# Sums of squares by row on ScalarE, and key stores on ScalarE's queue, in the first stage of a hybrid attention kernel

## The chip, the cores and the metric

One core of a Trainium2 chip runs the whole layer as one program. The metric is device time in microseconds, the median of several executions; a lower time is better. The engines are TensorE (PE, with its weight loads PEld), VectorE (DVE), ScalarE (ACT), GpSimd (POOL) and SyncE (SP, which here only issues DMAs). Each engine works through its own list in program order and stands still when the next instruction has to wait.

## The reference

The layer takes 2048 latent tokens `x` and 256 context tokens `ctx`, each of width 1024. What matters here is its first part:

```python
def _rmsnorm(x, g):
    xf = x.astype(jnp.float32)
    xf = xf * lax.rsqrt(jnp.mean(xf * xf, axis=-1, keepdims=True) + EPS)
    return (xf * g.astype(jnp.float32)).astype(x.dtype)
...
        h_lat = _rmsnorm(x, norm_g[i]) * (1.0 + scale) + shift
        h_ctx = _rmsnorm(ctx, norm_g[i]) * (1.0 + scale_c) + shift_c
```

`shift` and `scale` come from a product of SiLU(c) with `w_ada`. The normalised and modulated tokens `h` are multiplied by the input projection `w_in` (queries, keys, values and gates of two groups of heads), then come neighbourhood attention, retention, the output projection, a residual and a last RMSNorm.

## The kernel before, in words

Tokens are held transposed: width on the partitions, tokens along the free dimension. They come in nine groups of 256 (0 to 7 are latent, 8 is the context), and two groups make a block of 512 (`blk[0]` to `blk[3]`; `blk[4]` is the context alone, 256 wide). A float32 value is carried as a high part (rounded by ScalarE to `fp32r`) and a low part (the difference, by VectorE or POOL), and each product is three matmuls: high by high, high by low, low by high.

The first stage, some 170 us, does two things at once. PE runs five windows (`window(b)`, L491), one for each block, in which it computes the keys of neighbourhood attention: four key units (`u_k`, L380) of 128 output columns, each with eight k-steps of three matmuls (`tform`, L357; the matmul is L363). A window so has 32 steps, and step n of window b has the number 32b + n. In the first window the four units are interleaved as `STEPS` says; in the others they come one after another. When a unit ends, ScalarE rounds its result into a tile `o` (L383), VectorE forms the low part (L384), and both are stored to DRAM in `kS` (L385). The pool `op` has two buffers for `o`. `store` (L149) defers the DMA by one `tick`, and the window calls `tick` right behind the unit's end, in the same step.

Between the steps stands the preparation of later blocks. `PLAN` (L39) lists it by hand, with the step after which each action is emitted, in the order of the list. For a group i, the actions are: `x`, load the transposed tokens (`load_x`, L182); `sq`, squares on ScalarE (L198), folded from eight k-tiles to one by adds on POOL and VectorE (L200, L201, L203); `cs`, the sum over the partitions by matmuls with a column of ones (L209); `rs`, r = (mean + eps)^-0.5, a scale on VectorE (L214) and a power on POOL (L215), and its copy to 128 columns on VectorE (L220); `sp`, the spread of r over the partitions by matmuls with the identity (L227); `mu`, the tokens times r, on VectorE in halves of four k-tiles (L241); `ab`, times scale plus shift, two k-tiles on VectorE (L272) and two on ScalarE (L274) for most groups; `hl`, the high part on ScalarE (L279) and the low part on VectorE or POOL as `LOV` says (L283). For groups 0 and 1, `p` does the last two by k-tile (`prep_first`, L255: L262 on ScalarE, L263 and L265). `s`, `m`, `ar` and `af` make the four quarters of `scale` and `shift` (L298, L311, L319, L324 to L332). Prepared tokens are also spilled to DRAM in `hS` for later stages (L253, on SP's queue, eight steps behind `hl`), and from there they come back at L516.

The pool `st` has four buffers of 128x1024 float32. They hold the raw weights of `ws` (`st_halves`, L172), the squares of groups 2 to 8 and the raw tokens of group 8, in turn. SP's queue carries all loads, the spills and, up to the last window, the key stores; in window 4 the queue for the stores becomes ScalarE's (L495).

Of the kernel before, what the change touches and what calls it, by code (L numbers as in the profile page):

```python
# [9 lines left out]
F32 = mybir.dt.float32  # L10
BF16 = mybir.dt.bfloat16
F32R = mybir.dt.float32r
AF = mybir.ActivationFunctionType
# [69 lines left out]
def hybrid_kernel(ctx: ExitStack, tc: tile.TileContext, a: dict, out: bass.AP):  # L83
# [47 lines left out]
    env = dict(pp=pool(psx, "pp", 6, space=PSUM), st=pool(sx, "st", 4, side="right"), queue=nc.sync)  # L131
# [61 lines left out]

    def squares(i):
        sqs[i] = []
        for u in range(2):
            sq = xsq[i][u] if i < 2 else env["st"].tile([P, KH, 256], F32, name="st")
# [7 lines left out]
    def colsum(*ii):  # L205
        pm = ptile(None if ii[0] < 4 else psm)
        for j, i in enumerate(ii):
            for t in range(2):
                nc.tensor.matmul(pm[:, 2 * j + t:2 * j + t + 1], sqs[i][0][:, 0, t * P:(t + 1) * P], one, start=True, stop=True)  # L209
            rms[i] = pm[:, 2 * j:2 * j + 2]  # L210

    def rstd(i):
        r = env["st"].tile([P, 2], F32, name="rs", bufs=4)
        nc.vector.tensor_scalar(r, rms[i], 1.0 / D, EPS, ALU.mult, ALU.add)  # L214
# [3 lines left out]
    def spread_copy(i):  # L218
        rbs[i, 1] = env["st"].tile([P, 2, P], F32, name="t0", bufs=2)
        nc.vector.tensor_copy(rbs[i, 1], rbs[i].unsqueeze(2).to_broadcast([P, 2, P]))  # L220
# [95 lines left out]
    def ada_row(u):  # L316
        rows[u] = op.tile([P, 2, 512], F32, name="o")[:, 0, :]
        n = 4 if SPL[u] else 2
        (nc.scalar.copy, nc.vector.tensor_copy)[u % 2](rows[u][0:n, :], aps[u][0:n, :])  # L319
# [1313 lines left out]
```

## Time and profile before

| what | us |
|---|---|
| median of 3 runs (1350.23 to 1353.26) | 1350.68 |
| the profiled execution | 1347.8 |
| its span | 1345.9 |
| PE busy | 1304.7 |
| PEld busy | 1145.7 |
| DVE busy | 834.6 |
| ACT busy | 606.3 |
| POOL busy | 578.9 |

The profile is of one execution. A row of a timeline gives the start, the length, the engine, the line, the operation and its tiles, and in brackets how long the engine had stood before it and what ended that. A row of the groups gives the count, the busy time and the mean in ns, and behind the second bar the idle time ahead of the group by what ended it. A row of the waits gives who waited for whom: us in total, times, longest.

### The profile page before, as it was taken

What the parts mean: (1) busy time and instruction counts of PE and PEld (TensorE: products, weight loads), DVE (VectorE), ACT (ScalarE), POOL (GpSimd) and SP (SyncE); (2) the same over time, 40 slices, a digit from 0 to 9 for tenths busy, and PEclk for the clock granted to TensorE, in tenths of its full rate; (3) what the DMA queues carried; (4) which work ended last, traced back from release to release, by engine and by line L of the source; (5) the groups of instructions that cost most, each with busy time, mean ns of one, the idle gap of its engine ahead of it and who ended that gap; (6) DMA issues with size and microseconds to landing.
All of it is one profiled execution on the core that took longest, in us unless ns stands there. A gap on an engine that the chain in (4) does not pass through costs nothing.

```text
span 1345.9 us, 23104 instructions
## 1 busy us (share of the span) xinstructions
PE 1304.7 (97%) x8236; PEld 1145.7 (85%) x8236; DVE 834.6 (62%) x1444; ACT 606.3 (45%) x1259; POOL 578.9 (43%) x569
## 2 busy tenths in 40 slices
PE   6989999999999999999999999999999999999997
PEld 2477899878898888998999889889999788888886
DVE  5786356776676754477767777776654734444445
ACT  5454333243533343555655465556642244333432
POOL 5452102555104664354535465655533154544442
PEclk9999999999999999999999999999999999999999
DMA  9386788565867657967587876766547888445533
GB/s 363 139 281 235 266 301 219 185 223 184 315 184 230 213 177 239 265 199 198 146 227 210 225 225 205 192 183 192 167 149 250 277 297 275 158 157 172 165 127 125
DMA packets 172086, 287.26 MB, mean 213 GB/s; under 512 B 17345, under 2 KB 92225, under 8 KB 170690
## 3 DMA queue, kind: packets, MB, share of 16 engines
q1 hardware_dynamic: 139554, 228.35, 56.2%
q10 hardware_dynamic: 32416, 57.42, 11.9%
q8 instruction: 66, 1.08, 0.3%
q14 instruction: 50, 0.41, 0.1%
HBM read 194.48 MB, written 91.23 MB: 212 GB/s over the span
## 4 chain that ended last, share of the span: by engine, by line
PE 79%; DVE 6%; DMA 5%; ACT 3%; POOL 3%; issue 2%; SPq 0%; ACTq 0%; POOLq 0%; DVEq 0%
PE mm L374 21%; PE mm L671 17%; PE mm L1474 11%; PE mm L363 7%; PE sS L1034 5%; PE tr L1061 3%; PE po L1082 3%; PE mm L1196 2%; PE tr L1063 2%; PE po L1084 2%; PE mm L311 2%; PE mm L1386 1%; PE mm L1385 1%; PE mm L1384 1%; DMA v<-rvS 1%
## 5 line engine op out<-in xcount | busy, mean ns | idle before, releaser
L374 PE MATMUL mm<-whi,hlo 128*128 128x256 f32 x832 | 228.5, 282 | 1.0 <-DMA hlo<-cS 1.0
L374 PE MATMUL mm<-whi,hhi 128*128 128x256 f32 x768 | 224.2, 292 | 0.0
L374 PE MATMUL mm<-wlo,hhi 128*128 128x256 f32 x768 | 216.8, 282 | 0.0
L1065 ACT CAST pt<-tr 128x640 fp32r<-128x640 f32 (+1 forms) x128 | 95.7, 747 | 160.0 <-PE tr L1063 157.4
L1071 DVE TENSOR_TENSOR pt<-tr,pt 128x640 fp32r<-128x640 f32 (+1 forms) x128 | 113.9, 890 | 78.7 <-ACT pt L1065 77.5
L374 PEld LDWEIGHTS mm<-whi,hlo 128*128 128x128 f32 x832 | 156.5, 191 | 1.4 <-DMA hlo<-cS 1.3
L1054 POOL TENSOR_SCALAR sp<-sp,stt 128x640 f32<-128x640 f32 (+2 forms) x128 | 103.7, 812 | 106.3 <-DVE stt L1053 77.3
L374 PEld LDWEIGHTS mm<-whi,hhi 128*128 128x128 f32 x768 | 146.3, 190 | 0.1
L374 PEld LDWEIGHTS mm<-wlo,hhi 128*128 128x128 f32 x768 | 146.1, 190 | 0.0
L625 POOL TENSOR_TENSOR whi<-st,whi 128x512 fp32r<-128x512 f32 x48 | 64.6, 1367 | 160.2 <-ACT whi L624 159.3
L1043 DVE CUSTOM_DVE_ANT_0 sp<-sS,nb 128x640 f32<-128x640 f32 (+2 forms) x128 | 105.6, 825 | 34.1 <-PE sS L1034 27.7
L1048 ACT ACTIVATE sp<-sp,stt 128x640 f32<-128x640 f32 (+2 forms) x128 | 107.4, 839 | 20.0 <-DVE stt L1043 18.8
L363 PE MATMUL mm<-hhi,whi 128*128 128x512 f32 x256 | 107.4, 419 | 0.0
L363 PE MATMUL mm<-hlo,whi 128*128 128x512 f32 x256 | 101.1, 395 | 6.4 <-DVE hlo L283 2.3
L1034 PE MATMUL sS<-k,q 128*128 128x256 f32 (+3 forms) x512 | 99.1, 315 | 5.3 <-DVE stt L1043 5.1
L363 PE MATMUL mm<-hhi,wlo 128*128 128x512 f32 x256 | 101.2, 395 | 0.3 <-DVE wlo L347 0.3
L671 PE MATMUL mm<-hhi,whi 128*128 128x512 f32 x336 | 97.4, 394 | 0.0
L1474 PE MATMUL mm<-wor,y 128*128 128x512 f32 x384 | 95.6, 398 | 1.3 <-DVE xt L1483 1.2
L1483 DVE TENSOR_TENSOR xt<-mm,xt 128x512 f32<-128x512 f32 x64 | 43.8, 686 | 82.7 <-PE mm L1474 82.7
L1034 PEld LDWEIGHTS sS<-k,q 128*128 128x128 f32 x512 | 82.7, 188 | 12.3 <-DVE stt L1043 8.6
L1474 PE MATMUL mm<-won,y 128*128 128x512 f32 x336 | 89.9, 406 | 0.0
L1474 PEld LDWEIGHTS mm<-wor,y 128*128 128x128 f32 x384 | 69.9, 188 | 17.4 <-issue 3.4
(258 smaller groups left out, 3034.8 us busy)
## 6 DMA issues: line engine op xcount, KB each, us to landing
st<-in_w_in_dram SPq DMA_DIRECT2D x64, 512.0 KB
q<-qS SPq DMA_DIRECT2D x64, 256.0 KB
hlo<-hS SPq DMA_DIRECT2D x20, 512.0 KB
k<-kS SPq DMA_DIRECT2D x16, 576.0 KB
kS<-o SPq DMA_DIRECT2D x16, 512.0 KB
vB<-o SPq DMA_DIRECT2D x64, 128.0 KB
qS<-o ACTq DMA_DIRECT2D x16, 512.0 KB
woS<-g ACTq DMA_DIRECT2D x32, 256.0 KB
```

What stands on the lines that cost most here:

```text
L363: nc.tensor.matmul(pm[:, :n], ww[:, k, cs], h[:, k, :], start=(k == 0 and i == 0), stop=(k == KC - 1 and i == 2))
L374: nc.tensor.matmul(pm[:, t * WG:(t + 1) * WG], h[:, k, o:o + P], ww[:, k, :], start=(k == 0 and i == 0), stop=(k == KC - 1 and i == 2))
L625: nc.gpsimd.tensor_tensor(t[:, 1], r, f(t)[:, 0], ALU.subtract)
L671: nc.tensor.matmul(pm, ww[:, k, :], hh[:, k, :], start=(k == 0 and i == 0), stop=(k == KH - 1 and i == 2))
L1034: nc.tensor.matmul(o, hd["q"][i][:, hl, j * P:(j + 1) * P], k, start=(hl == 0), stop=(hl == 1))
L1043: nc.vector.tensor_tensor_reduce(T["sp"][:, :n], T["s"], nbz[big][:, o:o + n], -1.0, 3e38, ALU.add, ALU.min, T["st"][:, 0:1])
L1048: nc.scalar.activation(sp[:, :n], sp[:, :n], AF.Exp, bias=st[:, 0:1], scale=-1.0, accum_out=st[:, 1:2])
L1054: nc.gpsimd.tensor_scalar(sp[:, :n], sp[:, :n], st[:, 2:3], 0.0, ALU.mult, ALU.add)
L1065: nc.scalar.copy(pt[:, :ng_ + 2, 0, :], tr[:, :ng_ + 2, :])
L1071: nc.vector.tensor_tensor(pt[:, :n, 1, :], tr[:, :n, :], f(pt)[:, :n, 0, :], ALU.subtract)
L1474: nc.tensor.matmul(pm, yy[:, k, :], ww[:, k, sl], start=(k == 0 and i == 0), stop=(k == 3 and i == 2))
L1483: nc.vector.tensor_tensor(xts[t][:, sl], pm, xts[t][:, sl], ALU.add)
```

## The change

Its own summary reads: "Row-wise sums of squares on ScalarE for groups two to eight, with five and six in ScalarE's gap, r on POOL, and key stores on ScalarE's queue one unit later."

For groups two to eight the sum of squares is taken by rows. A new action `xt` loads the group's tokens a second time, untransposed, as two tiles of 128 tokens by 1024, into the buffers of `st`; `squares` is then one ScalarE instruction for each tile, which squares in place and accumulates along the row into a column of `rms`. The folding adds and the column sums of these groups are gone. The scale of `rstd` and the copy of `spread_copy` go from VectorE to POOL for these groups. The rows `ar` of quarters two and three are copied by VectorE (quarter two was ScalarE's). Key stores go on ScalarE's queue in all windows. `PLAN` is written anew: groups two and three load and are squared a few steps from where they were, groups four to eight are squared earlier (five and six at step 18, between the two halves of groups two and three), and the preparation of groups two and three moves from steps 16 to 29 to steps 14 to 22.

```diff
-    (12, 'p', 5), (12, 'm', 3, 1), (12, 'p', 4), (13, 'sq', 4), (13, 'cs', 2, 3), (13, 'm', 3, 2), (14, 'm', 3, 3),
-    (15, 'rs', 2), (15, 'ar', 3), (16, 'rs', 3), (16, 'af', 3), (16, 'sp', 2, 3), (17, 'mu', 3, 0), (18, 'p', 7),
...
+    (-1, 'p', 1), (-1, 'm', 1, 3), (-1, 'ws', 1), (0, 'ar', 1), (3, 'af', 1), (4, 'xt', 2), (4, 'xt', 3), (4, 'mu', 1, 1),
+    (4, 's', 2, 0), (4, 'x', 4), (4, 'p', 2), (7, 'm', 2, 0), (8, 'm', 2, 1), (9, 'p', 3), (9, 'sq', 2), (9, 'sq', 3),
+    (9, 'm', 2, 2), (9, 'm', 2, 3), (9, 'ar', 2), (10, 'xt', 4), (10, 'x', 5), (11, 'xt', 5), (12, 'mu', 0, 1),
+    (12, 'af', 2), (12, 'm', 3, 0), (12, 'p', 5), (12, 'm', 3, 1), (12, 'p', 4), (12, 'rs', 2), (12, 'rs', 3),
+    (13, 'm', 3, 2), (13, 'm', 3, 3), (13, 'ar', 3), (14, 'sp', 2, 3), (14, 'mu', 2, 0), (14, 'mu', 3, 0), (14, 'sq', 4),
+    (14, 'blk', 1), (15, 'xt', 6), (16, 'af', 3), (17, 'rs', 4), (17, 'p', 7), (18, 'p', 6), (18, 'x', 6),
+    (18, 'ab', 2, 0), (18, 'ab', 3, 0), (18, 'hl', 2, 0), (18, 'hl', 3, 0), (18, 'sq', 5), (18, 'sq', 6),
+    (18, 'mu', 2, 1), (18, 'mu', 3, 1), (19, 'ab', 2, 1), (20, 'ab', 3, 1), (21, 'hl', 2, 1), (22, 'hl', 3, 1),
+    (26, 'sp', 4), (28, 'mu', 4, 0), (30, 'mu', 4, 1), (30, 'rs', 5), (30, 'rs', 6), (30, 'xt', 7), (36, 'ab', 4, 0),
+    (38, 'x', 7), (41, 'sq', 7), (42, 'ab', 4, 1), (44, 'rs', 7), (45, 'blk', 2), (46, 'hl', 4, 1), (46, 'hl', 4, 0),
+    (46, 'xt', 8), (50, 'sp', 5), (50, 'x', 8), (51, 'mu', 5, 0), (52, 'mu', 5, 1), (53, 'ab', 5, 0), (54, 'ab', 5, 1),
+    (55, 'hl', 5, 0), (55, 'blk', 3), (58, 'hl', 5, 1), (61, 'sq', 8), (68, 'sp', 6), (70, 'rs', 8), (73, 'mu', 6, 1),
...
-    env = dict(pp=pool(psx, "pp", 6, space=PSUM), st=pool(sx, "st", 4, side="right"), queue=nc.sync)
+    env = dict(pp=pool(psx, "pp", 6, space=PSUM), st=pool(sx, "st", 4, side="right"), queue=nc.scalar)
...
+    def load_xt_(i):
+        sqs[i] = []
+        src = a["ctx"] if i == 8 else a["x"][i * 256:(i + 1) * 256, :]
+        for t in range(2):
+            xt = env["st"].tile([P, KH, 256], F32, name="st").rearrange("p k t -> p (k t)")
+            nc.sync.dma_start(xt, src[t * P:(t + 1) * P, :])
+            sqs[i].append(xt)
+
     def squares(i):
+        if i >= 2:
+            rms[i] = env["st"].tile([P, 2], F32, name="rs", bufs=4)
+            for t, xt in enumerate(sqs[i]):
+                nc.scalar.activation(xt, xt, AF.Square, accum_out=rms[i][:, t:t + 1])
+            return
...
-        nc.vector.tensor_scalar(r, rms[i], 1.0 / D, EPS, ALU.mult, ALU.add)
+        r = rms[i] if i >= 2 else env["st"].tile([P, 2], F32, name="rs", bufs=4)
+        (nc.gpsimd if i >= 2 else nc.vector).tensor_scalar(r, rms[i], 1.0 / D, EPS, ALU.mult, ALU.add)
...
-        nc.vector.tensor_copy(rbs[i, 1], rbs[i].unsqueeze(2).to_broadcast([P, 2, P]))
+        (nc.gpsimd if i >= 2 else nc.vector).tensor_copy(rbs[i, 1], rbs[i].unsqueeze(2).to_broadcast([P, 2, P]))
...
-        (nc.scalar.copy, nc.vector.tensor_copy)[u % 2](rows[u][0:n, :], aps[u][0:n, :])
+        (nc.scalar.copy, nc.vector.tensor_copy)[u > 0](rows[u][0:n, :], aps[u][0:n, :])
...
-            if b == 4 and n == 0:
-                env["queue"] = nc.scalar
```

More of the change, by code (lines that the diff above doesn't have):

```diff
@@ L192, in hybrid_kernel @@
     sqs, rms, rbs, prs = {}, {}, {}, {}
-    def squares(i):
+    def load_xt_(i):
[5 more added lines that the diff above has]
+            sqs[i].append(xt)
+    def squares(i):
+        if i >= 2:
[3 more added lines that the diff above has]
+            return
         sqs[i] = []
         for u in range(2):
-            sq = xsq[i][u] if i < 2 else env["st"].tile([P, KH, 256], F32, name="st")
+            sq = xsq[i][u]
             nc.scalar.activation(sq, raw[i][u], AF.Square)
@@ L205, in colsum @@
     def colsum(*ii):
-        pm = ptile(None if ii[0] < 4 else psm)
+        pm = ptile()
         for j, i in enumerate(ii):
@@ L212, in rstd @@
     def rstd(i):
-        r = env["st"].tile([P, 2], F32, name="rs", bufs=4)
-        nc.vector.tensor_scalar(r, rms[i], 1.0 / D, EPS, ALU.mult, ALU.add)
+        r = rms[i] if i >= 2 else env["st"].tile([P, 2], F32, name="rs", bufs=4)
+        (nc.gpsimd if i >= 2 else nc.vector).tensor_scalar(r, rms[i], 1.0 / D, EPS, ALU.mult, ALU.add)
         nc.gpsimd.tensor_tensor(r, r, mhalf[:, 0:2], ALU.pow)
@@ L466, in hybrid_kernel @@
         lds[name](*args)
-    acts = dict(sq=squares, cs=lambda *i: colsum(*i), rs=lambda i: (rstd(i), spread_copy(i)), sp=lambda *i: spread(*i),
+    acts = dict(sq=squares, xt=load_xt_, cs=lambda *i: colsum(*i), rs=lambda i: (rstd(i), spread_copy(i)), sp=lambda *i: spread(*i),
                 mu=lambda i, u: spread_mul(i, (u,)), ab=prep_ab, hl=prep_hl, blk=alloc_blk, x=load_x, w=lambda: wr.append(w_raw(2560)),
```

20 rows, old and new, of the table PLAN are left out of this document.

## The prediction

> **What bounds the kernel now.** I read the page's busy shares first, then the windows of the first 170 us (the only stretch that the diff touches), then who TensorE (PE) waited for in that stretch, and last the timelines of the engines around each of those waits.
>
> ```profile
> span 1345.9 us, 23104 instructions
> PE 1304.7 (97%) x8236; PEld 1145.7 (85%) x8236; DVE 834.6 (62%) x1444; ACT 606.3 (45%) x1259; POOL 578.9 (43%) x569
> ```
> PE is busy 97% of the span, so only what shortens PE's own list or its few holes can help. The holes lie early:
> ```profile
> 27.00:72.00 45.00, 42.19 (x166) 23.51 (x165) 34.32 (x61) 22.66 (x36) 22.41 (x20) 1.00 0.43 171
> 72.00:100.00 28.00, 24.20 (x111) 19.55 (x111) 24.71 (x33) 14.64 (x20) 14.63 (x8) 1.00 0.98 328
> ```
> The columns are PE, PEld, DVE, ACT, POOL, clock, DMA share, GB/s. From 72 to 100 us VectorE is busy 24.7 of 28 and the DMA engines 98%; ScalarE (ACT) has about half its time free. PE's waits from 27 to 170 us:
> ```profile
> PE mm L363 <- DVE hlo L283: 2.3, 2, 2.0
> ...
> PE mm L227 <- DVE t L220: 1.5, 1, 1.5
> PE mm L363 <- POOL hlo L283: 1.5, 1, 1.5
> PE mm L374 <- DVE wlo L347: 0.8, 1, 0.8
> PE mm L374 <- ACT whi L345: 0.6, 1, 0.6
> ```
> These rows hold 6.7 us. A block of 512 tokens cannot start before its low parts (L283) are written, so preparation sets these stretches, one "gate" at the second half of block 1 and one at the start of block 2:
> ```profile
> 77.43 0.47 PE L363 MATMUL mm<-hlo,whi 128*128 128x512 f32 x1 [0.39 <-DVE hlo L283]
> ...
> 99.62 0.50 PE L363 MATMUL mm<-hlo,whi 128*128 128x512 f32 x1 [1.46 <-POOL hlo L283]
> ...
> 105.06 0.71 PE L227 MATMUL mm<-ident,t 128*128 128x128 f32 x4 [1.50 <-DVE t L220]
> 105.52 0.48 PE L363 MATMUL mm<-hhi,whi 128*128 128x512 f32 x1
> ```
> The question is when these gates open in the changed kernel.
>
> **Part 1: the column sums go from PE.** L209 over groups two to eight:
> ```profile
> L209 PE MATMUL mm<-one,st 128*128 128x1 f32 x28 | 3.6, 237 | 0.4 <-DVE st L203 0.4
> ```
> At most 4.0 us. But five of the seven groups' sums (two to six) lie ahead of the 99.62 gate; if that gate opens when preparation is done, they are absorbed. Only seven and eight, behind it, are sure: 8 of 28 matmuls (about 1.0) with the 0.4 of waiting and some 0.2 of restart, **-1.6 us**.
>
> **Part 2: VectorE and POOL are relieved.**
> ```profile
> L200 DVE TENSOR_TENSOR st<-st 128x512 f32<-128x512 f32 x7 | 5.7, 819 | 0.9 <-ACT st L198 0.9
> L241 DVE TENSOR_TENSOR hlo<-hlo,mm 128x1024 f32<-128x1024 f32 x4 | 4.8, 1213 | 0.5 <-PE mm L227 0.5
> ...
> L201 DVE TENSOR_TENSOR st<-st 128x256 f32<-128x256 f32 x7 | 3.8, 547 | 0.2
> L220 DVE COPY t<-rs 128x256 f32<-128x256 f32 x7 | 3.1, 445 | 5.7 <-POOL rs L215 5.7
> ```
> ```profile
> L201 POOL TENSOR_TENSOR st<-st 128x256 f32<-128x256 f32 x7 | 5.8, 830 | 0.5
> ```
> VectorE loses L200, L201 and L220: 12.6 us of work and 6.8 of waiting (L241 stays; its 1.2 is used below). POOL loses adds of its own and gets, beside its power, a scale and the copy; the copy is bounded by VectorE's 0.45 and POOL's 0.83 for an add of that size, so I take 2 us for all of r in a group. It is ready before its spread:
> ```profile
> 58.75 1.34 PE L227 MATMUL mm<-ident,t 128*128 128x128 f32 x8
> ```
> That old spread of two and three comes two steps (1.4 us), one transposition (0.3) and the column sums (0.9) earlier, at 56.1; their squares end by 47.2 (part 4) and r by 54, with POOL's low parts of k-tile 5 ahead of it. So r is not on the path, and the 1.5 us at L227 goes. The relief matters also because the two engines shut each other out:
> ```profile
> 72.72 1.21 DVE L283 TENSOR_TENSOR hlo<-hlo,hhi 128x1024 fp32r<-128x1024 f32 x1
> 73.86 0.68 DVE L384 TENSOR_TENSOR o<-mm,o 128x512 fp32r<-128x512 f32 x1
> 74.46 2.83 DVE L283 TENSOR_TENSOR hlo<-hlo,hhi 128x1024 fp32r<-128x1024 f32 x1
> ```
> ```profile
> 73.36 2.84 POOL L283 TENSOR_TENSOR hlo<-hlo,hhi 128x1024 fp32r<-128x1024 f32 x1 [1.68 <-ACT hhi L279]
> ```
> The same subtraction takes VectorE 1.21 us alone, and 2.83 when it has to wait for POOL's to end at 76.2; POOL's 2.84 holds half a us of the same waiting (until 73.9), so 2.4 alone.
>
> **Part 3: ScalarE's list.** It keeps its squares, now with a read of the accumulator behind each, and gets the key stores. Its prices:
> ```profile
> 59.64 2.08 ACT L262 ACTIVATE hhi<-hhi,mods 128x256 fp32r<-128x256 f32 x4 [7.87 <-DVE mods L332]
> ...
> 67.17 1.09 ACT L274 ACTIVATE hlo<-hlo,mods 128x256 f32<-128x256 f32 x2
> 68.16 1.04 ACT L279 CAST hhi<-hlo 128x1024 fp32r<-128x1024 f32 x1
> 69.10 1.09 ACT L274 ACTIVATE hlo<-hlo,mods 128x256 f32<-128x256 f32 x2
> ...
> 74.62 2.01 ACT L198 ACTIVATE st<-hhi 128x1024 f32<-128x1024 f32 x2
> 80.67 0.59 ACT L383 CAST o<-mm 128x512 fp32r<-128x512 f32 x1 [4.04 <-DMA kS<-o]
> 83.56 0.59 ACT L383 CAST o<-mm 128x512 fp32r<-128x512 f32 x1 [1.31 <-DMA kS<-o]
> ...
> 153.57 0.60 ACTq L151 DMA_DIRECT2D kS<-o  x1
> ```
> ```profile
> 1154.38 0.65 ACT L1430 ACTIVATE ot<-xt 128x512 bf16<-128x512 f32 x1
> 1154.90 0.22 ACT L1430 ACTIVATION_READ_ACCUMULATOR ot<-xt 128x1 f32 x1
> 1154.99 0.64 ACT L1302 CAST y<-y 128x512 fp32r<-128x512 f32 x1
> ```
> From start to start: a pair of modulations 1.0, a cast 0.95, a square 1.0 and the read behind it 0.09 (at worst its whole 0.22), so 2.1 us a group (2.4 at worst). A key unit now takes cast 0.6, then ScalarE stands until VectorE has written the low part (0.68), then issues for 0.55: 1.9 instead of 0.5, sixteen times. Everything behind it on ScalarE (modulations, high casts) stands too.
>
> The output tiles are two, so a cast also waits for the store two units before. The stores of the second and third unit:
> ```profile
> 74.56 0.54 SPq L151 DMA_DIRECT2D kS<-o  x1
> ...
> 79.04 0.53 SPq L151 DMA_DIRECT2D kS<-o  x1
> ```
> They landed at 80.67 and 83.56 (the waits above): 6.1 and 4.5 us. I take 4.5, because the changed kernel spills its first block and loads group six ahead of 72 us, which takes load from the stretch that is 98% full; bounds 3.5 (one us under the shorter row) and 6.1.
>
> Here a rule speaks against the change. The Trainium skill, "DMA: Bandwidth & Descriptors", section "Issuing engines are not separate DMA queues", says that DMAs started by any engine run on the same 16 DMA engines, and that another issuer saves only the issuing. By it the landing stays at 4.5 to 6.1 us and the 3.5 falls out. The rows above cannot decide it, as none shows a key store on ScalarE's queue in a stretch like this one.
>
> **First gate.** PE's pace, from the chain of waits (24 matmuls are eight steps, so 0.70 a step):
> ```profile
> 82.58 5.59 PE mm L363 x24
> ```
> In the old trace ScalarE starts k-tiles 6 and 7 at 59.64. The new one does at about 59.85 (VectorE now multiplies groups two and three first). Then: those four activations 2.0, four modulations 2.0, two casts 1.9, giving 65.7; squares five and six 4.2, giving 69.9. VectorE meanwhile writes a low part after POOL's (68.4), then multiplies the second halves (1.2 each) by 70.8, so the squares indeed fill a gap. Modulations until 71.9, casts until 73.8, POOL's low part 72.9 to 75.3 and VectorE's behind it to **76.5**. Old: 77.4.
>
> **Second gate.** Behind that stand four key units, waiting for VectorE at 76.5. Stores issue at 77.2 and 79.1; the third cast waits for 77.2 + 4.5 = 81.7 and stores at 83.0; the fourth for 79.1 + 4.5 = 83.6, stores at 84.9, free at 85.45. A modulation pair to 86.4; block 1's first unit waits for 83.0 + 4.5 = 87.5, free at 89.35. Square seven 2.1, modulations 1.0, casts 1.9: 94.35. Next unit's cast and low part to 95.6; VectorE's two multiplications to 98.0, the modulations behind them to 99.0, cast to 100, POOL's low part 2.4 to 102.4. The start of block 2, where PE needs only the high part at first, comes at **102.2**; PE alone would be there at 76.5 + 28 steps of 0.70 + 0.5 for a spread = 96.6, so it stands 5.6 us. Old: 99.62, and the old step five steps on, behind a spread, is at 105.52 (with the 1.5 at L227); the new one reaches that point at 102.2 + 5 x 0.70 + 0.46 = 106.1, **+0.6 us**. Each us of landing counts twice here: 3.5 gives -1.4, 6.1 gives +3.8.
>
> **Part 4: loads.** 14 more loads of 512 KB. The DMA view from 0 to 60 us, in 40 slices:
> ```profile
> GB/s 0 115 235 407 396 399 303 421 415 355 418 410 401 412 412 410 410 404 418 410 404 412 410 404 415 407 415 410 401 382 38 5 0 5 0 0 0 0 0 0
> ```
> The queue is empty after slice 31, near 46 us. Rows of groups two and three take the places that groups four and five had at the end of this queue, so they land by 46 and the squares are done by 47.2, ahead of the modulation rows that ScalarE waits for next. Cost nothing; the cover is the DMA share of 0.43 up to 72 us. Should it be gone, PE would wait at the spread near 56, after 5 us of slack.
>
> **Part 5: the tail.**
> ```profile
> 163.58 0.37 ACT L383 CAST o<-mm 128x256 fp32r<-128x256 f32 x1 [4.60 <-DMA kS<-o]
> ```
> The 0.8 and 0.6 before L374 come from this wait for the key store of 153.57, which shares the DMA engines with reloads of spilled tokens. SyncE no longer stands behind key stores, so the reloads start earlier: between -1.4 and 0; I take the middle, **-0.7**.
>
> **Sum.** +0.6 - 1.6 - 0.7 = -1.7 us. The profiled execution took 1347.8 (span 1345.9), so 1346.1 there; it lay 2.9 below the median of 1350.68, which becomes **1349.0**. A measurement of this kernel tells about 0.2% (2.7 us) from no change, so this is no change.
>
> **Rivals.** *Faster: the second gate opens before PE comes.* Then PE reaches block 2 at 96.6, passes the old 105.52 at 100.6, and with -1.6 the kernel gains 6.5 us: 1344.2. For it: VectorE alone loses 19 us of work and waiting in a stretch where it held PE, and ScalarE is half free. Against: ScalarE's list above, in order, with no gap left. Between this and the forecast lie landings under 4 us.
>
> *Slower: ScalarE becomes the bound.* With landings of 6.1 us the second gate costs +3.8 instead of +0.6; and block 3's gate, where ScalarE has four key units of 1.9 and 8 us of preparation in 17 us, slips 1.6: together, without the tail's gain, +3.8 + 1.6 - 1.6 = +3.8, 1354.5. It decides from a landing of about 5.5 us, or from squares at 2.4. For it: 98% DMA share, and the row of 6.1.
>
> *The change does less than it says.* Its summary puts the key stores "one unit later"; no line of the diff does. The store is deferred by one tick, and the tick follows in the same step. If it were one unit later, 0.68 of standing would go from each of the six units above, about -4 us: 1345. I give that 0.03.
>
> **Chances.** Forecast 0.40, faster rival 0.34, slower rival 0.23, the last 0.03. The forecast's own range (landing 4 to 5, tail -1.4 to 0) is 1347.3 to 1350.7. The full range reaches to both rivals and 2 us beyond the fast one, since other holes may close too: 1342 to 1355. Faster by over 0.2%: 0.40; within: 0.36; slower: 0.24.
>
> **What would show it.** Right: no L209 after 30 us; the wait at L227 gone; PE's largest wait at the start of block 2 for POOL's L283, 4 to 7 us; ScalarE's casts L383 idle for key stores between 77 and 90 us, and its stores following VectorE's low parts directly; block 1's second gate at 76 to 78. Wrong: block 2 starting under 98 us with no wait (the faster rival), PE standing for the spread of groups two and three (loads late), or a new wait at block 3.

## The result, and the profile after

The changed kernel takes **1361.82 us** (median of 7 runs, 1357.95 to 1367.22) where the kernel before takes 1352.92 beside it (7 runs, 1348.39 to 1354.63): a ratio of 1.0071, 95% interval 1.0047 to 1.0094, so 0.7% slower. The forecast was 1349.0, the range 1342 to 1355. The profiled execution of the changed kernel took 1359.81 us.

The first lines of its page:
```profile
span 1358.0 us, 23049 instructions
PE 1308.2 (96%) x8208; PEld 1148.0 (85%) x8208; DVE 814.9 (60%) x1410; ACT 607.6 (45%) x1272; POOL 565.6 (42%) x569
```
The span is 12.1 us longer; PE is busy 3.5 us longer with 28 instructions fewer. VectorE and POOL are 20 and 13 us lighter, as the change wanted. Line numbers behind the helper functions move on by 11 to 13: L283 is now L296 (low part), L279 L292 (high cast), L274 L287, L383 L396 (cast of a key unit), L384 L397, L363 L376, L374 L387, L345 L358.

The windows of the changed kernel, with the columns as before (PE, PEld, VectorE, ScalarE, POOL, clock, DMA share, GB/s):
```profile
72.00:100.00 28.00, 23.44 (x96) 18.39 (x94) 11.79 (x15) 11.39 (x18) 8.63 (x11) 0.94 0.87 293
100.00:127.00 27.00, 21.37 (x83) 16.99 (x84) 17.64 (x24) 11.87 (x19) 6.92 (x6) 0.81 0.56 203
```
VectorE fell from 24.7 to 11.8 us of 28, and yet PE does less there: 83 instructions against 113 from 100 to 127 us, and its clock, 1.00 in these windows of the kernel before, is 0.81. Where PE stood, from its timeline:
```profile
76.54 0.47 PE L376 MATMUL mm<-hlo,whi 128*128 128x512 f32 x1 [2.17 <-POOL rs L227]
...
103.99 0.79 PE L376 MATMUL mm<-hhi,whi 128*128 128x512 f32 x1 [6.30 <-ACT hhi L292]
106.42 0.80 PE L376 MATMUL mm<-hlo,whi 128*128 128x512 f32 x1 [1.64 <-POOL hlo L296]
...
170.82 0.58 PE L387 MATMUL mm<-whi,chi 128*128 128x256 f32 x1 [3.46 <-ACT whi L358]
```
The first gate opens at 76.5, to the tenth where it was forecast (the name POOL is of a step long done: VectorE's low part ends at 76.39). Block 2 starts at 103.99 where 102.2 was forecast (old: 97.78), and its low part comes at 106.42 (old: 99.62). The first product L387 comes at 170.82, 9.7 us after the old 161.1, and the stage behind it starts at 242.9 instead of 232.0. So the loss has two places, block 2's gate and the end of window 3: the first product behind the spread of group six, five steps into block 2, comes at 112.42 instead of 105.52, which is 6.9 us, and by 171 us it is 9.7 of the 12.1.

ScalarE's timeline ahead of block 2 (ACTq rows are its DMA issues):
```profile
73.71 0.58 ACT L396 CAST o<-mm 128x512 fp32r<-128x512 f32 x1
77.02 0.63 ACTq L151 DMA_DIRECT2D kS<-o  x1
77.70 0.58 ACT L396 CAST o<-mm 128x512 fp32r<-128x512 f32 x1 [3.41 <-DVE o L397]
79.04 0.52 ACTq L151 DMA_DIRECT2D kS<-o  x1
85.45 0.59 ACT L396 CAST o<-mm 128x512 fp32r<-128x512 f32 x1 [7.16 <-DMA kS<-o]
86.79 0.52 ACTq L151 DMA_DIRECT2D kS<-o  x1
87.41 0.59 ACT L396 CAST o<-mm 128x512 fp32r<-128x512 f32 x1 [1.37 <-DMA kS<-o]
```
The stores are issued at 77.0 and 79.0, as forecast (77.2, 79.1). But the third cast waits until 85.45 for the first and the fourth until 87.41 for the second: **8.4 us each**, where 4.5 was taken and 6.1 was the upper bound. (In f0_after below, the same kernel again, the first takes 7.5.) What the DMA engines did there, in windows of 4 us:
```profile
72.00:76.00 4.00, 2.29 (x9) 1.31 (x7) 2.16 (x1) 2.29 (x3) 2.97 (x2) 1.00 1.08 385
76.00:80.00 4.00, 3.46 (x10) 2.77 (x11) 3.80 (x5) 0.58 (x1) 2.82 (x6) 0.67 1.05 384
80.00:84.00 4.00, 4.00 (x18) 3.23 (x17) 0.14 (x1) 0.00 (x0) 0.00 (x0) 0.91 0.98 362
84.00:88.00 4.00, 4.00 (x19) 3.30 (x18) 0.69 (x1) 1.18 (x2) 0.00 (x0) 1.00 0.17 61
```
They are full until 84 us and nearly idle behind it. Of the 1.05 MB of the two stores 0.90 had moved by then; the last 0.15 took until 87, and no run shows why these went so slowly. The clock column, the third from the end, also shows 0.67 just after the first gate.

### The profile page after: what moved, and what is told of

It is laid out like the page before. It is cut to its first block, busy times and chain, and to the rows that moved or that the text cites. A ratio compares the mean times of both kernels' runs of the same rounds, so it can differ in the third digit from the quotient of the medians.

```text
span 1358.0 us, 23049 instructions
## 1 busy us (share of the span) xinstructions
PE 1308.2 (96%) x8208; PEld 1148.0 (85%) x8208; DVE 814.9 (60%) x1410; ACT 607.6 (45%) x1272; POOL 565.6 (42%) x569
## 3 DMA queue, kind: packets, MB, share of 16 engines
q8 instruction: 65, 1.06, 0.3%
## 5 line engine op out<-in xcount | busy, mean ns | idle before, releaser
L387 PE MATMUL mm<-whi,hlo 128*128 128x256 f32 x832 | 228.5, 282 | 0.8 <-DMA hlo<-cS 0.8
L387 PE MATMUL mm<-whi,hhi 128*128 128x256 f32 x768 | 224.2, 292 | 0.0
L387 PE MATMUL mm<-wlo,hhi 128*128 128x256 f32 x768 | 216.8, 282 | 0.0
L1082 DVE TENSOR_TENSOR pt<-tr,pt 128x640 fp32r<-128x640 f32 (+1 forms) x128 | 113.8, 889 | 78.5 <-ACT pt L1076 77.3
L387 PEld LDWEIGHTS mm<-whi,hlo 128*128 128x128 f32 x832 | 156.3, 190 | 1.2 <-DMA hlo<-cS 1.1
L387 PEld LDWEIGHTS mm<-whi,hhi 128*128 128x128 f32 x768 | 146.1, 190 | 0.0
L387 PEld LDWEIGHTS mm<-wlo,hhi 128*128 128x128 f32 x768 | 145.9, 190 | 0.0
L376 PE MATMUL mm<-hhi,whi 128*128 128x512 f32 x256 | 108.9, 425 | 7.4 <-ACT hhi L292 6.3
L376 PE MATMUL mm<-hlo,whi 128*128 128x512 f32 x256 | 102.8, 402 | 5.6 <-POOL rs L227 2.2
L376 PE MATMUL mm<-hhi,wlo 128*128 128x512 f32 x256 | 102.8, 402 | 0.3 <-DVE wlo L360 0.3
L1045 PEld LDWEIGHTS sS<-k,q 128*128 128x128 f32 x512 | 82.7, 188 | 12.1 <-DVE stt L1054 8.4
```

The source lines that it names most:

```text
L376: nc.tensor.matmul(pm[:, :n], ww[:, k, cs], h[:, k, :], start=(k == 0 and i == 0), stop=(k == KC - 1 and i == 2))
L387: nc.tensor.matmul(pm[:, t * WG:(t + 1) * WG], h[:, k, o:o + P], ww[:, k, :], start=(k == 0 and i == 0), stop=(k == KC - 1 and i == 2))
L1045: nc.tensor.matmul(o, hd["q"][i][:, hl, j * P:(j + 1) * P], k, start=(hl == 0), stop=(hl == 1))
L1082: nc.vector.tensor_tensor(pt[:, :n, 1, :], tr[:, :n, :], f(pt)[:, :n, 0, :], ALU.subtract)
```

## Experiments

Each kernel is named by its label; its ratio is to the kernel before on the same chip, with the 95% interval. "L387" is the start of the first product of that line (before 161.1, after 170.8), the place where nearly all that the diff touches is over. It is read from one profiled execution, so a us or two of it can be chance. Kernels with the same first letter were measured together on one chip. From letter to letter the ratios are the better comparison, as the median of the kernel before itself went from 1349.6 to 1352.9 us.

| kernel | what it is | median us | ratio | L387 |
|---|---|---|---|---|
| e1_sync | change, key stores of windows 0 to 3 on SyncE | 1354.70 | 1.0039 [1.0026, 1.0052] | 166.7 |
| e2_act | before, all key stores on ScalarE | 1370.97 | 1.0160 [1.0146, 1.0173] | 183.8 |
| e3_later | change, stores one unit later | 1364.12 | 1.0114 [1.0100, 1.0129] | 174.3 |
| e4_fill | change, 26 unread products ahead of block 2 | 1358.34 | 1.0063 [1.0051, 1.0076] | 169.7 |
| f0_after | change, again | 1360.23 | 1.0089 [1.0069, 1.0109] | 170.3 |
| f1_tail | change, window 3's stores on SyncE | 1355.15 | 1.0041 [1.0025, 1.0056] | 165.9 |
| f2_later_loads | change, groups 7, 8 later in the plan | 1356.38 | 1.0055 [1.0039, 1.0070] | 166.4 |
| f3_halves_later | e1_sync, second halves of groups 2, 3 later | 1348.15 | 0.9988 [0.9976, 1.0000] | 157.5 |
| g1_halves_act | change, second halves later | 1359.48 | 1.0073 [1.0057, 1.0090] | 168.8 |
| g2_both_later | f3 with f2's edit | 1352.78 | 1.0014 [1.0004, 1.0025] | 163.4 |
| g3_squares_back | f3, squares 5, 6 at their old steps | 1350.50 | 0.9998 [0.9985, 1.0012] | 162.0 |
| g4_warm | f3, 12 unread products ahead of block 1 | 1347.70 | 0.9974 [0.9964, 0.9984] | 158.7 |
| h1_loads_held | change, loads of group 7 behind a spill | 1351.48 | 0.9997 [0.9983, 1.0011] | 164.1 |
| h2_held_and_tail | h1 and f1's edit | 1350.64 | 0.9990 [0.9974, 1.0006] | 157.5 |
| h3_warm_both | g4, 12 more ahead of block 2 | 1345.48 | 0.9955 [0.9941, 0.9969] | 156.9 |
| h4_fill | change, 12 and 30 ahead of blocks 1, 2 | 1357.44 | 1.0037 [1.0023, 1.0052] | 170.9 |
| i1_scalar_warm | h2, 12 each ahead of blocks 1, 2 | 1349.51 | 0.9985 [0.9976, 0.9995] | 157.8 |
| i2_warm_again | h3, again | 1345.67 | 0.9961 [0.9949, 0.9974] | 158.2 |

### Is it ScalarE's queue?

**e1_sync** changes only where the key stores are issued.
```diff
-    ... queue=nc.scalar)
+    ... queue=nc.sync)
+            if b == 4 and n == 0:
+                env["queue"] = nc.scalar
```


> The changed kernel with the key stores back on SyncE's queue up to the last window; everything else of the change stays. Theory 1 (the stores on ScalarE's queue share the DMA engines with spills and loads instead of standing ahead of them in one queue, land late, and ScalarE waits for them and for VectorE's low parts): the first product of block 2 comes at 99 us or earlier instead of 104.0, the wait before the context's second set of units falls from 4.0 to under 1.5 us, and the median is 8 us or more under that of the changed kernel (1344 to 1353). Theory 2 (ScalarE's list itself is too long, with the squares moved ahead, whatever queue stores): block 2 still starts after 102 us and the median stays above 1357.

It won 4 to 7 us, but not where the first theory had it. PE's timeline of e1_sync, and ScalarE's:
```profile
104.16 0.79 PE L376 MATMUL mm<-hhi,whi 128*128 128x512 f32 x1 [6.16 <-ACT hhi L292]
```
```profile
81.43 0.59 ACT L396 CAST o<-mm 128x512 fp32r<-128x512 f32 x1 [6.36 <-DMA kS<-o]
...
92.81 0.59 ACT L396 CAST o<-mm 128x512 fp32r<-128x512 f32 x1 [5.55 <-DMA kS<-o]
```
Block 2 stands as long as before. The first store, issued at 77.33 with the loads of group seven now behind it, lands in 4.1 us. But the third leaves SyncE only at 85.52, behind spills and loads, and takes 7.3: the delay has moved from the first stores to the third. The first theory falls for the gate; the second falls for the sum, as the end of window 3 did come sooner.

**e2_act** is the other half: the kernel before with `queue=nc.scalar` from the start.

> The kernel before with its key stores on ScalarE's queue from the first window on, nothing else. Theory 1: slower by 5 to 10 us (1356 to 1363), ScalarE's casts wait 15 us or more for key stores. Theory 2: within 2.7 us of the kernel before, since its list without the early squares has room.

It costs 21 us, twice what the first theory gave at most. ScalarE's timeline shows how:
```profile
83.89 0.52 ACTq L151 DMA_DIRECT2D kS<-o  x1
84.45 2.01 ACT L198 ACTIVATE st<-hhi 128x1024 f32<-128x1024 f32 x2 [4.44 <-DVE o L384]
```
The 4.44 us before the square are the stand ahead of the store, with its issue: ScalarE waits until VectorE, which in the kernel before has 24.7 us of work in these 28, has written the low part. In the changed kernel, with VectorE relieved, the same stand is 1.3 us but for the first store. So the relief of VectorE pays for a part of what the queue costs.

**e3_later** takes the change's summary at its word: `store(kS[...], f(o)[:, :, :n], 2)`.

> The changed kernel with each key store issued one unit later, still on ScalarE's queue, as its summary says. ScalarE no longer stands for VectorE's low part (0.7 us, six units ahead of block 2), but each store also starts later. Theory 1 with the landing as the main cost: landings of 8 us remain, block 2 starts within 2 us of 104, median within 3 us of 1361.8. Rival within theory 1 (the standing is the main cost): block 2 starts at 100 us or earlier and the median falls by 4 us or more.

It is the slowest version of the change: the store now follows ScalarE's next cast, which itself waits for an earlier store. Its casts wait 7.81, 5.57 and 5.20 us, and block 2 starts at 107.93, later than either theory had it.

### Is it the clock?

**e4_fill** keeps PE busy ahead of block 2 with products that nobody reads.
```diff
+            if b == 2 and n == 0:
+                pd = ptile()
+                for e in range(26):
+                    nc.tensor.matmul(pd, w01[0][0][:, 0, 0:P], blk[1][0][:, 0, :], start=(e == 0), stop=(e == 25))
```


> The changed kernel with 26 more products (5.9 us of PE) ahead of block 2, whose result nobody reads, so that PE does not stand there. Theory: the products after the 6.3 us gap run at 0.43 us instead of 0.23 for 4 us because the granted clock is down after a long stand; then the fill costs nothing, the products of block 2 run at 0.23 from the start, and the median falls by 2 us (1359 to 1360.5). Rival (the products are slow because something else feeds them slowly): they stay at 0.43 and the median stays or rises.

**h4_fill** does the same, 12 products ahead of block 1 and 30 ahead of block 2.

> The changed kernel with twelve unread products ahead of block 1 and thirty ahead of block 2, so that PE does not stand in either gate; nothing else is changed. Theory 'the clock': the slower products cost 2 us behind each gate, of which the first is covered by the stand at block 2; block 2's gate stays at 103 to 106, the spread of group eight comes at 131 to 132 instead of 133.9, and the median lies 1.5 to 3 us under the changed kernel's. Rival 'only the gate counts': it stays within 1 us of it.

In h4_fill the products behind block 1's gate run at full pace: the clock is 1.00 from 76 to 84 us. At block 2 the filling falls short. PE's timeline of h4_fill:
```profile
103.49 0.50 PE L376 MATMUL mm<-hhi,whi 128*128 128x512 f32 x1 [0.72 <-ACT hhi L292]
105.92 0.50 PE L376 MATMUL mm<-hlo,whi 128*128 128x512 f32 x1 [1.93 <-POOL hlo L296]
...
107.56 0.63 PE L376 MATMUL mm<-hlo,whi 128*128 128x512 f32 x1
107.99 0.63 PE L376 MATMUL mm<-hhi,wlo 128*128 128x512 f32 x1
...
131.74 0.50 PE L376 MATMUL mm<-hlo,whi 128*128 128x512 f32 x1 [0.65 <-DVE hlo L296]
170.88 0.58 PE L387 MATMUL mm<-whi,chi 128*128 128x256 f32 x1 [4.73 <-ACT whi L358]
```
PE still stands 0.72 us, does one product and stands 1.93, and from 107.2 to 110.6 us products start 0.43 us apart again (full pace is 0.23). e4_fill is alike, with stands of 0.61 and 1.94. So neither run is a full test of the clock at block 2. What h4_fill shows is that block 1's slow products are covered by the next gate: without them block 2 starts at 103.49 (f0_after 103.63). Block 3's gate is no earlier than preparation lets it (131.74, f0_after 132.38), and at L387 nothing is left: 170.88 against 170.3. The ratios, 1.0063 and 1.0037 against 1.0089 and 1.0071 for the two measurements of the change, leave room for 1 to 7 us; what the clock costs the change in all stays open.

### The end of window 3

**f0_after** is the changed kernel again, for comparison on the same chip; **f1_tail** puts window 3's four stores back on SyncE's queue.
```diff
+            if n == 0:
+                env["queue"] = nc.sync if b == 3 else nc.scalar
```


> The changed kernel again, unaltered, as the yardstick of the three beside it: a ratio to the kernel before of 1.005 to 1.009, block 2's first product at 104 us.

> The changed kernel, with the four key stores of window 3 alone on SyncE's queue (window 4's and those of windows 0 to 2 stay on ScalarE's). Theory 'lost place': about 4.5 us of the loss come after window 3, because the last key store lands among the reloads of hS that SyncE issued just before it, where SyncE's queue would have put it ahead of them. Then the cast after it no longer waits 8.8 us, the last stretch comes 4 us sooner, and the median lies 3 to 5 us under the changed kernel's; block 2 still starts at 104. Rival 'everything is the gate': the tail only inherits the 6 us that block 2 lost, and the median falls by less than 1 us.

f1_tail wins 5.1 us (6.5 by the ratios) and lands at e1_sync's time (1355.15, 1354.70), though the stores of windows 0 to 2 are on ScalarE's queue in it and on SyncE's in e1_sync. So of these stores only window 3's counted for the sum, although block 2 also starts 1.0 us sooner in f1_tail (102.59). In the changed kernel ScalarE's timeline has
```profile
157.30 0.52 ACTq L151 DMA_DIRECT2D kS<-o  x1
...
168.00 0.37 ACT L396 CAST o<-mm 128x256 fp32r<-128x256 f32 x1 [8.78 <-DMA kS<-o]
169.72 1.99 ACT L358 CAST whi<-st 128x1024 fp32r<-128x1024 f32 x2 [1.35 <-DVE o L397]
```
10.7 us from issue to landing, with the weight split that PE waits for behind it. SyncE had issued four reloads (2 MB) at 156.21. What each queue moved (packets, MB, share), in the stretches 157 to 162 and 162 to 168 us (q1 is SyncE's; q10, which moves nothing around the gates of f3_halves_later, where SyncE issues the stores, is ScalarE's):
```profile
q1 hardware_dynamic: 324, 1.20, 91.2%
```
```profile
q1 hardware_dynamic: 384, 1.38, 59.2%
q10 hardware_dynamic: 533, 0.78, 34.6%
```
Nothing of the store moves for its first 4.7 us. In f1_tail SyncE issues it ahead of the reloads:
```profile
156.07 0.53 SPq L151 DMA_DIRECT2D kS<-o  x1
156.69 2.41 SPq L529 DMA_DIRECT2D hhi<-hS  x4
```

### What makes block 2 late

**f2_later_loads** moves the loads and squares of groups seven and eight to later steps.
```diff
-    (30, 'xt', 7), ... (38, 'x', 7), (41, 'sq', 7), ... (44, 'rs', 7), ... (46, 'xt', 8), ... (50, 'x', 8), ... (61, 'sq', 8), ... (70, 'rs', 8),
+    (50, 'xt', 7), ... (53, 'x', 7), ... (62, 'sq', 7), (64, 'rs', 7), (64, 'xt', 8), (66, 'x', 8), ... (74, 'sq', 8), (76, 'rs', 8),
```


> The changed kernel, with the loads of group seven (2 MB in both layouts) and of group eight 8 to 20 steps later, the squares of seven and eight later with them; the stores and ScalarE's order up to block 2 stay. Theory 'crowding': the first key stores land in 8.4 us because SyncE's loads of x^T seven and the spills fill the DMA engines from 72 to 84. Then the third cast of a key unit comes at 81.5 to 83.5 instead of 85.5, block 2's first product at 101.5 to 102.5 and the median falls by 2 to 4 us. Rival 'the spills alone suffice', or the stretch behind is crowded by the moved loads instead: the third cast after 84, block 2 after 103.5, the median within 1 us of the changed kernel's.

The third cast still comes at 85.37. But the experiment missed its mark, as SyncE's timeline shows:
```profile
72.17 2.20 SPq L199 DMA_DIRECT2D st<-in_x_dram  x2
74.48 0.93 SPq L190 DMA_DIRECT2D clo<-in_xT_dram  x2
```
A plan step only sets the order on SyncE; with nothing to wait for, it issued the loads at 72 to 75 us all the same. The spills ahead of them are out by 72.1, and the store still takes 8.6 us, so it is not the spills. What f2 won came from ScalarE, where the squares of seven (2.1 us) no longer stand ahead of group four's casts (93.31, f0_after 96.02).

**f3_halves_later** goes for the order: second halves behind window 0's key units, as in the kernel before, with e1's queue.
```diff
-    (18, 'mu', 2, 1), (18, 'mu', 3, 1), (19, 'ab', 2, 1), (20, 'ab', 3, 1), (21, 'hl', 2, 1), (22, 'hl', 3, 1),
+    (22, 'mu', 2, 1), (23, 'mu', 3, 1), (26, 'ab', 2, 1), (28, 'ab', 3, 1), (29, 'hl', 2, 1), (29, 'hl', 3, 1),
```


> The changed kernel, with all key stores of windows 0 to 3 on SyncE again (as in e1_sync), and with the second halves of groups two and three (multiplication, modulation, split) at the steps that they had before (22 to 29 instead of 18 to 22), behind window 0's first key units. Theory 'bunching': the gate of block 2 is late because window 0's casts to o stand behind both second halves on ScalarE, so that all key stores leave after 77 us and compete. Then the first key cast comes at 66 to 70 us, the first store leaves by 71, block 1 starts at 77 to 79, block 2 at 99.5 to 101, and the median lies within 1.5 us of the kernel before. Rival 'the moved loads': the stores still land in over 5 us between 77 and 90, block 2 starts after 103, and the median stays 4 to 6 us over the kernel before.

All of the loss is gone. From its timelines, SyncE's first store and PE's gate:
```profile
70.30 0.62 SPq L151 DMA_DIRECT2D kS<-o  x1
```
```profile
99.94 0.50 PE L376 MATMUL mm<-hlo,whi 128*128 128x512 f32 x1 [0.96 <-POOL hlo L296]
```
The first store leaves 6.7 us sooner than in the change, ahead of the spills and loads. It keeps the row sums, the gap and r on POOL, and lies 0 to 0.24% under the kernel before: about what the forecast gave for these parts. A store is late here too: the third, issued by SyncE at 78.08, lands at 86.12, after 8.0 us. But only block 1's first cast waits for it (6.47 us), since window 0's four casts are done by 78.7, and block 2 is in time. So a late landing costs what stands behind it, whatever queue it came from.

**g1_halves_act** makes that edit alone, stores still on ScalarE.

> The changed kernel with the second halves of groups two and three later (steps 22 to 29, as in f3_halves_later) and nothing else: all key stores stay on ScalarE's queue. Theory 'two separate losses': the plan's order costs some 6.5 us (block 2's gate), window 3's last key store on ScalarE's queue some 5 us, and they add. Then block 2 starts at 100 to 101.5, the last stretch still waits 3 us or more for the weight split behind the key store, and the median lies 4 to 6 us over the kernel before. Rival 'the order is only right with SyncE': ScalarE, held by VectorE's low part ahead of each store, delays the second halves behind it, block 2 starts after 103, and the median lies 8 us or more over the kernel before.

The rival holds: block 2 starts at 103.14 (its low part at 105.56), and the kernel takes 8.3 us more than the one before. PE's timeline:
```profile
77.41 0.80 PE L376 MATMUL mm<-hhi,whi 128*128 128x512 f32 x1 [4.03 <-ACT hhi L292]
```
Block 1 now waits, as ScalarE stands for VectorE ahead of each store with the second halves behind it. So the early halves of the change's plan are what the queue asked for: order and queue belong together, and the two losses do not simply add.

**h1_loads_held** holds the 2 MB of group seven back for good, behind a spill that isn't ready before 89 us; group eight's loads and squares move behind them.
```diff
-    (30, 'xt', 7), ... (38, 'x', 7), (41, 'sq', 7), ...
+    (58, 'xt', 7), (58, 'x', 7), ... (66, 'sq', 7), (68, 'rs', 7), (68, 'xt', 8), (70, 'x', 8), ... (78, 'sq', 8), (80, 'rs', 8),
```


> The changed kernel with the loads of group seven in both layouts (2 MB) issued behind the first spill of group four, and the squares of seven and eight later with them. Theory 'crowding': with these loads 2 MB less go through the DMA engines between 67 and 84 us; what is left behind 72 us, two spills and two key stores of 0.5 MB each, takes 5.5 us at 375 GB/s, so the first key store lands by 81, the third cast comes at 80 to 82 instead of 84 to 85.5, block 2's first product at 98 to 101.5, and the median lies 3 to 6 us under the changed kernel's 1360. Rival 'a store on ScalarE's queue is slow by itself': the third cast still comes after 83.5.

This is the decisive one. Its windows, ScalarE's third cast and PE's gate:
```profile
76.00:80.00 4.00, 3.38 (x10) 2.69 (x11) 3.84 (x5) 0.59 (x1) 2.90 (x6) 0.69 0.36 131
```
```profile
77.10 0.58 ACTq L151 DMA_DIRECT2D kS<-o  x1
...
81.23 0.59 ACT L396 CAST o<-mm 128x512 fp32r<-128x512 f32 x1 [2.90 <-DMA kS<-o]
```
```profile
99.24 0.50 PE L376 MATMUL mm<-hlo,whi 128*128 128x512 f32 x1 [1.24 <-POOL hlo L296]
```
The same store from the same queue at the same time lands in 4.1 us instead of 8.4, the DMA share is 0.36 instead of 1.05, block 2's low part is 7 us sooner, and the kernel is as fast as the one before: 0.9997 against f0_after's 1.0089, some 12 us (8.8 by the medians, which are of two chips). At block 2's low part some 3 us come from the squares of seven, as in f2_later_loads (103.35 there), and the other 4.1 from the loads, as spills and squares are alike in the two. Both stores have moved all of their bytes by 83 us. So the queue alone does not make a store late; 2 MB of loads ahead of it do.

**h2_held_and_tail** adds f1's edit.

> The kernel of h1_loads_held with window 3's four key stores on SyncE's queue, as in f1_tail. Theory 'two separate losses': crowding ahead of block 2 and the lost place at the end of window 3 add, and the median lies 4 to 6 us under h1_loads_held, within 3 us of the kernel before. Rival 'one is inside the other': with block 2 in time the tail costs nothing, and the median stays within 1.5 us of h1_loads_held.

0.9990 against 0.9997: here the rival is right, the tail gives nothing more that can be measured, although L387 comes 6.6 us sooner in its profile. The two profiled executions cannot be compared for that: h1's was the slowest of its 12 runs (1356.76), h2's among its fastest (1346.79).

**g2_both_later** adds f2's edit to f3.

> The kernel of f3_halves_later (stores of windows 0 to 3 on SyncE, second halves later) with the loads and squares of groups seven and eight later too, as in f2_later_loads. Theory 'crowding': it moves stores and spills apart, block 2 starts by 99 and blocks 2 and 3 meet no wait over 0.5 us, 1 us or more under f3_halves_later. Rival 'the weights are next': whatever is won before 157 us is lost again between 157 and 190, where products wait for the splits of the next weights, and the median stays within 1 us of f3_halves_later.

Neither was right: block 2 has no wait, but block 3 has a new one, 4.08 us at 125.92 for ScalarE's high cast. Ahead of it ScalarE does the later squares (2.1 us), and ahead of these it had stood 8.66 us until 116.79, by the trace for a key store; which of the two made the cast late was not separated.

### Squares in the gap

**g3_squares_back** returns squares five and six to steps 31 and 52 (and `xt` seven to 32, so that it has its buffer).

> The kernel of f3_halves_later with the row-wise squares of groups five and six back at steps 31 and 52, where the kernel before had its squares of these groups. Theory 'the gap is free': moved into ScalarE's idle time they take 4.2 us from the stretch of block 1, where the casts are; put back, ScalarE's casts in block 1 and the mods of group five come later, block 2 starts 0.5 to 2 us later, the median 0 to 2 us over f3_halves_later. Rival 'they are in the way at 65.7 us': the gate of block 1 waits for the casts behind these squares; put back, block 1 starts at 74 to 75 instead of 76.5, and the median falls by 1 to 2 us.

The first gate stays (76.68), so the rival falls; block 2's low part comes at 101.77 instead of 99.94. The times cannot be told apart. So the move into the gap costs nothing that can be seen, and may be worth a us.

### A version that beats both

**g4_warm** and **h3_warm_both** give f3 unread products ahead of the gates, as in e4_fill; **i2_warm_again** repeats the second, and **i1_scalar_warm** gives h2 the same.

> The kernel of f3_halves_later with twelve products of 512 columns that nobody reads ahead of block 1, in the stand of 73.8 to 76.5 us. Theory 'the clock': the products of 0.43 us instead of 0.23 from 77 to 82 us follow from the stand; without it they take 0.23 us from the gate on, block 1's units end 2 us earlier, and block 2's start or the end of window 3 comes 1 to 2 us sooner. Rival 'covered': block 2 starts when ScalarE and POOL have its operands, so that block 1's sooner end only makes the stand ahead of block 2 longer, and the median does not move by more than 0.7 us.

> The kernel of g4_warm with twelve unread products ahead of block 2 as well. Theory 'the clock': the products after block 2's start, 0.43 us in g4_warm's trace for some 5 us, take 0.23 us, and the median falls by another 1 to 2 us, to 1345 to 1347 (0.995 to 0.9965 of the kernel before). Rival 'the weights are next': the median stays within 0.8 us of g4_warm's ratio of 0.9974.

> The kernel of h2_held_and_tail (key stores of windows 0 to 2 on ScalarE's queue, loads of group seven held, window 3's stores on SyncE) with twelve unread products ahead of blocks 1 and 2. Theory 'the queue itself is free': without the crowding it does as well as h3_warm_both, a ratio of 0.9945 to 0.9965. Rival 'the issue on ScalarE costs': ScalarE stands 1.3 to 1.4 us for VectorE ahead of each store, and the ratio lies at 0.997 or above.

> h3_warm_both again, unaltered, as the yardstick of i1_scalar_warm: a ratio of 0.994 to 0.997 to the kernel before.

h3's windows:
```profile
72.00:100.00 28.00, 26.81 (x120) 21.62 (x119) 15.23 (x23) 14.02 (x22) 12.02 (x12) 1.00 1.03 360
100.00:127.00 27.00, 27.00 (x123) 22.01 (x122) 15.34 (x21) 12.74 (x21) 3.69 (x4) 1.00 0.76 280
```
The clock is 1.00 throughout (f3: 0.88 from 72 to 100), and the version is a little faster than both kernels: 0.3 to 0.6% under the kernel before, and 0.26 to 0.51% when repeated. g4's interval overlaps that of f3, h3's does not; and the slow products go where PE no longer stands, so the stands are their cause. i1 reaches only 0.9985, against 0.9961 for i2 on one chip, 3.8 us by the medians. The rival holds in size, but not in its cause: the two reach L387 together (157.8 and 158.2), and all of the difference comes behind it, where the key stores are on ScalarE's queue in both. There i1 has PE's largest stand, for the weight split, and a clock of 0.85 from 157 to 180 us where i2 has 1.00:
```profile
166.49 0.39 PE L387 MATMUL mm<-whi,chi 128*128 128x256 f32 x1 [2.80 <-ACT whi L358]
```
So up to 158 us the change's queue and order cost nothing that can be seen, once the loads are held, the stands are filled and window 3's stores are on SyncE. What makes the weight split late in i1 stays open.

## Why the prediction was wrong

**The step that failed** is Part 3's landing of the key stores: "I take 4.5, because the changed kernel spills its first block and loads group six ahead of 72 us, which takes load from the stretch that is 98% full; bounds 3.5 ... and 6.1". It measured 8.4, twice (7.5 in f0_after for the first). The mechanism (two output tiles, each cast waiting for the store two units before) was right, the premise was not: into the place of what had moved ahead came group seven, 2 MB in both layouts. Its plan steps 30 and 38 look late, but a step is only a place in SyncE's order; SyncE had nothing to wait for and issued these loads at 66.86 and 73.56, where the kernel before, whose queue stood behind key stores, issued x^T seven at 91.31. Without them the store lands in 4.1 us (h1_loads_held) and the forecast's own 4.5 would have been 0.4 too high.

**The upper bound** was too low, though a row of the kernel before shows more. 6.1 was the worst store on SyncE's own queue. The store of 153.57 in Part 5 went on ScalarE's queue, behind four reloads on SyncE's, and the cast waited for it until 163.58: 10.0 us, for half the bytes. Part 3 says that no row shows such a store "in a stretch like this one", and left it out of the bounds.

The rule "each us of landing counts twice" held only once: the stores of the second round went into the idle stretch behind 84 us, and the first of them landed in 4.4 (86.79 to 91.16). So the 3.9 us of the landing made block 2's low part 4.0 us late, 106.42 instead of 102.4.

**Left out** was PE's clock after a stand. Part 3 counts 0.70 us a step behind a stand of 5.6; PE ran at half its clock there. The point that was forecast for 106.1 came at 112.42: 4.0 us of that are the low part, the other 2.3 the slow products.

**Part 5** had the wrong sign. That the reloads no longer stand behind key stores was right; but a reload ahead of the store is 2 MB ahead of it. -0.7 was forecast; f1_tail gives 5.1 us back, although in a kernel whose block 2 is in time the same edit gives nothing that can be measured (h2).

**Right:** Part 1 and Part 2 (the wait at the spread is gone, r is ready long before), the order and times on ScalarE until 79 us, the first gate at 76.5 (its steps came as listed, so this is no luck), the price of a square with its read (1.04 to 1.06 from start to start), loads that cost nothing ahead of 60 us. What f3 keeps of Parts 1 and 2 is worth 0 to 3.2 us; -1.6 was forecast for the surest of them.

**The rivals.** "ScalarE becomes the bound" named the right side and the right wait, with its point of decision at a landing of 5.5 us, but its 1354.5 stood on 6.1 us of landing, and it had only 0.23. "One unit later" forecast -4 us; as e3_later it makes the kernel slower still (1.0114).

**Where the 9 to 12 us are:** by the ratios, group seven's squares ahead of group four's casts make some 4.5 us (f2 against f0), crowding some 8 (h1 against f2; 4.9 by the medians), and the lost place in window 3 some 6.5 (f1 against f0; 5.1 by the medians). That is more than there is: h2 shows that the last overlaps with the others. How the rest divides, and what of it is the clock's, cannot be settled from these runs.

## What to carry to other kernels

A load placed late in a plan is late only if its queue has something to wait for: ask when it will be issued, not where it is listed, whenever a change takes waits out of that queue. A store that moves to another engine's queue loses its place ahead of the loads behind it, and that can cost more than the move saves. Price a landing by what else will be in flight in that stretch, not by the best rows of the old one.

## What the runs showed of the hardware

**A store on another queue gets nothing at first while the other queue fills the engines.** In the change, from 77 to 79 us and from 79 to 81 us, the queues moved
```profile
q1 hardware_dynamic: 375, 0.79, 108.1%
```
```profile
q1 hardware_dynamic: 161, 0.44, 59.2%
q10 hardware_dynamic: 151, 0.30, 38.9%
```
The store of 77.02 moves nothing for its first 2 us, then the two queues share about 3 to 2. In h1_loads_held, where SyncE's queue moves nothing from 77 to 83 us, the same store moves 0.24 MB up to 79. The Trainium skill, "DMA: Bandwidth & Descriptors", section "Issuing engines are not separate DMA queues", says that another issuer saves only the issuing: the trace agrees, as both queues' packets share the engines. Here the move also cost something: with the same plan the first store landed in 4.1 us from SyncE's queue (e1_sync), ahead of the loads, and in 8.4 from ScalarE's.

**PE runs at half its clock after some stands of about 2 us.** Behind the stand of 6.30 us, products of 512 columns start 0.43 us apart instead of 0.23:
```profile
107.01 0.63 PE L376 MATMUL mm<-hhi,wlo 128*128 128x512 f32 x1
107.44 0.63 PE L376 MATMUL mm<-hhi,whi 128*128 128x512 f32 x1
...
111.60 0.39 PE L376 MATMUL mm<-hlo,whi 128*128 128x512 f32 x1
111.82 0.40 PE L376 MATMUL mm<-hhi,wlo 128*128 128x512 f32 x1
```
That lasts some 5 us here and costs 2.3. It also came behind the stand of 2.17 us at 76.54, and in h4_fill behind a stand of 0.72, one product and a stand of 1.93. It did not come in the kernel before, behind the 1.96 at 74.08 and the 1.46 at 99.62, so the length of the stand alone does not decide. In the traces' records of the granted clock the slow stretches last 3.4 us or a multiple of it: in the change from 77.3 to 80.7 and from 101.2 to 111.5, in h4_fill from 107.2 to 110.7. The Trainium skill, "TensorE: Matmul & The Clock Gate", section "What's actually happening", has the clock at half after an idle window of about 3.4 us; half is what the trace shows, but 2.2 us of standing were enough here.
